# Up projections of a gated FFN as two-by-two blocks: seven products of half size in place of eight

## The chip, the cores and the metric

The kernel runs on one core of one Trainium2 chip, with its engines TensorE (PE in the profile), VectorE (DVE), ScalarE (ACT), GpSimd (POOL) and SyncE (SP, which issues most DMAs). The metric is device microseconds of one execution; runs are summed up by their median.

## The reference, cut to what matters

The program is a decoder trunk of two layers over 528 tokens (16 meta tokens and 512 real ones) of width 1024. Each layer is a token mixer (differential attention, then sparse attention with an indexer) followed by a gated FFN with a causal convolution of three taps. The FFN is the part that is changed:

```python
D_MODEL, FFN_HIDDEN, CONV_WIDTH = 1024, 2816, 3

def conv_ffn(h, w_up, conv_w, conv_b, w_down):      # h = rms_norm(stream, gain)
    u = h @ w_up                                    # 1024 x 5632
    T = u.shape[1]
    up = jnp.pad(u, ((0, 0), (CONV_WIDTH - 1, 0), (0, 0)))
    c = conv_b + sum(conv_w[j] * up[:, j:j + T] for j in range(CONV_WIDTH))
    g, val = jnp.split(c, 2, axis=-1)
    return (jax.nn.silu(g) * val) @ w_down          # 2816 x 1024
```

[...]

## The kernel before

Activations stand turned: 128 features on the partitions, 528 tokens along the free axis, so the stream h is eight tiles of 128 x 528. Every operand of a product is split into a rounded part and a rest (`two`, L392: ACT casts the high part, DVE or POOL subtracts it to get the low part), and a product is three matmuls: high by high, high by low, low by high. In the program's names the split weights are pairs wh and wl, or a lent pair of K tiles; the split activations are R tiles.

An up column is 128 columns of the weight: eight blocks of 128 x 128, each multiplied in three passes over two spans of tokens, 48 matmuls in all (`project`, L463). Column j of the gate half and column j of the value half make a pair; there are 22 pairs. `conv` (L924) takes a finished column out of PSUM: one DVE product with the row of inverse norms (tt<-ps,rbc), one ACT instruction for the last tap, two DVE instructions for the other taps (tt<-tt,cw,tt), then SiLU of the gate, the product of gate and value, and the split of the result into R tiles.

The columns come in three groups of 7, 7 and 8 pairs, and each is followed by its part of the down projection, eight products (`residual`, L699), whose PSUM result DVE adds to the stream (h<-ps,h). One pair of the next group is put ahead of each of the first two blocks of downs:

```python
order = ups[0] + ups[1][:2] + downs[0] + ups[1][2:] + ups[2][:2] + downs[1] + ups[2][2:] + downs[2]
```

What the text calls an up-block is the run of pairs between two blocks of downs: A (8 pairs), B (7) and C (7) in each layer.

A weight passes through two buffers. `loader` (L440) takes one of three raw tiles of 128 x 1024 and issues one DMA on the SP queue; `splitter` (L448) takes a wh/wl pair, casts and subtracts, and gives the raw tile back; `project` gives the pair back after its last matmul. There are two such pairs, and two more made of the attention's K tiles are lent while the FFN runs (`lend_keys`, L725). PSUM has four tiles of two banks, and columns take at most three of them (`PP`, L364).

The order on each engine is not written by hand. Tasks are generators with a priority; `Plan` (L192) emits the instruction that can start first by its own table of costs (`_cost`, L69) and keeps that order in the program. An instruction in an `Alt` may go to several engines, and the planner takes the one that ends first; `plan.bias` is added to DVE's end, and in the FFN it is `SPARE_FFN` (L52), 0 before the change, so that nearly all such instructions stand on DVE there.

## Time and profile before

| | |
|---|---|
| median of three runs | 1419.01 us (1418.5 to 1422.07) |
| the profiled execution | 1417.88 us, of which 1416.1 us lie between its first and last instruction |
| PE busy | 1372.6 us, 97% of the span, 10703 matmuls |
| DVE busy | 960.7 us, 68% |
| ACT busy | 679.9 us, 48% |
| POOL busy | 347.5 us, 25% |
| DMA | 124.33 MB, mean 88 GB/s |

The profile is of one execution. Busy time counts an instruction from its start to its end on its engine, waiting for a shared resource included; matmuls overlap, so their records are longer than their pace. A tile's name stands without its buffer number: tt is a work tile, ps a PSUM tile, raw and ns are tiles into which weights are loaded. In the trace every instruction has the line of the planner's emit (L270), so groups are told apart by tiles and shapes.

The two FFNs take the stretches from about 310 to 690 us and from about 1035 us to the end.

### The profile page before, as it was taken

The numbers are of one execution on the slowest core, as the hardware profiler recorded it, in microseconds if no ns is written. First come the engines' busy times: TensorE is split into PE (matmuls) and PEld (weight loads), VectorE is DVE, ScalarE is ACT, GpSimd is POOL, SyncE is SP. The second block draws the span as 40 slices with busy tenths as digits, with TensorE's granted clock in tenths as the row PEclk, the third lists the DMA queues.
The fourth block names the chain that finished last, engine by engine and source line by source line (L and its number), as shares of the span: only waits on it lengthen the run. The fifth ranks groups of instructions, "written<-read, shape, count | busy, mean of one in ns | idle before, by whom it ended". The sixth has DMA issues, their size and how long they took to land. (4 is left out here: it accounts for less than half of the span.)

```text
span 1416.1 us, 26368 instructions
## 1 busy us (share of the span) xinstructions
PE 1372.6 (97%) x10703; PEld 1331.9 (94%) x10703; DVE 960.7 (68%) x1659; ACT 679.9 (48%) x1260; POOL 347.5 (25%) x441
## 2 busy tenths in 40 slices
PE   8989999999999999999989989999999999999997
PEld 7888999999999999999989989898999989989997
DVE  6878767457645763775599988887666637646764
ACT  4566676434423432443356477777444324423454
POOL 1654654420000000000247764442310000000012
PEclk8999999999999999999999999999999999999999
DMA  6422233233233323332312331222333233333333
GB/s 178 103 61 61 76 91 103 57 96 90 81 95 94 87 82 102 90 90 70 90 45 75 83 96 49 69 68 76 94 90 97 80 104 92 91 101 90 90 113 111
DMA packets 223084, 124.33 MB, mean 88 GB/s; under 512 B 7001, under 2 KB 218338, under 8 KB 222962
## 3 DMA queue, kind: packets, MB, share of 16 engines
q1 hardware_dynamic: 219234, 111.89, 27.5%
q0 software_dynamic: 2560, 8.65, 2.9%
q10 hardware_dynamic: 1168, 2.10, 0.4%
q8 instruction: 84, 1.38, 0.4%
q14 instruction: 38, 0.31, 0.1%
HBM read 111.87 MB, written 2.10 MB: 80 GB/s over the span
## 5 line engine op out<-in xcount | busy, mean ns | idle before, releaser
L270 PE MATMUL ps<-R,wh 128*128 128x256 f32 (+4 forms) x4016 | 680.8, 289 | 1.6 <-POOL R L270 0.9
L270 PEld LDWEIGHTS ps<-R,wh 128*128 128x128 f32 (+1 forms) x4016 | 562.5, 189 | 9.4 <-POOL R L270 1.1
L270 PE MATMUL ps<-R,wl 128*128 128x272 f32 (+3 forms) x2008 | 424.4, 288 | 0.0
L270 PE MATMUL ps<-R,K 128*128 128x256 f32 (+3 forms) x3240 | 418.4, 289 | 0.0
L270 PEld LDWEIGHTS ps<-R,K 128*128 128x128 f32 x3240 | 405.6, 189 | 7.6
L270 PEld LDWEIGHTS ps<-R,wl 128*128 128x128 f32 x2008 | 312.2, 188 | 3.2
L270 ACT CAST wh<-raw 128x1024 fp32r<-128x1024 f32 (+3 forms) x173 | 145.6, 847 | 202.7 <-PE ps L270 147.6
L270 DVE TENSOR_TENSOR wl<-raw,wh 128x1024 fp32r<-128x1024 f32 (+3 forms) x128 | 139.9, 1096 | 23.6 <-ACT wh L270 21.8
L270 DVE TENSOR_TENSOR h<-ps,h 128x528 f32<-128x528 f32 (+3 forms) x70 | 45.7, 653 | 143.0 <-PE ps L270 143.0
L270 DVE TENSOR_TENSOR tt<-ps,rbc 128x528 f32<-128x528 f32 (+2 forms) x89 | 62.4, 701 | 114.9 <-PE ps L270 109.6
L270 DVE SCALAR_TENSOR_TENSOR tt<-tt,cw,tt 128x528 f32<-128x528 f32 (+1 forms) x176 | 133.4, 758 | 8.2 <-ACT tt L270 4.9
L270 ACT CAST K<-raw 128x1024 fp32r<-128x1024 f32 (+1 forms) x76 | 77.9, 1027 | 119.9 <-PE ps L270 105.5
L270 POOL TENSOR_TENSOR acc<-acc,tt 128x528 f32<-128x528 f32 (+1 forms) x22 | 36.2, 1645 | 400.6 <-ACT tt L270 400.6
L270 ACT CAST R<-tt 128x512 fp32r<-128x512 f32 (+2 forms) x84 | 48.5, 585 | 139.7 <-DVE tt L270 139.6
L270 DVE TENSOR_TENSOR K<-raw,K 128x1024 fp32r<-128x1024 f32 (+1 forms) x75 | 89.6, 1195 | 10.8 <-ACT K L270 9.3
L270 PE MATMUL ps<-K,X 128*128 128x272 f32 (+2 forms) x464 | 79.7, 308 | 11.0 <-DVE tt L270 5.6
L270 ACT ACTIVATE ns<-ns,st 128x528 f32<-128x528 f32 (+4 forms) x160 | 82.1, 514 | 13.6 <-DVE st L270 11.8
L270 POOL TENSOR_TENSOR wl<-raw,wh 128x512 fp32r<-128x512 f32 (+1 forms) x45 | 70.4, 1566 | 47.6 <-ACT wh L270 47.0
L270 PEld LDWEIGHTS ps<-K,X 128*128 128x128 f32 x464 | 65.6, 182 | 15.9 <-DVE st L270 3.9
L270 ACT ACTIVATE tt<-tt,cw 128x528 f32<-128x528 f32 (+1 forms) x88 | 72.3, 821 | 14.8 <-DVE tt L270 14.6
L270 POOL MEMSET tt<- 128x2 f32 x44 | 4.2, 99 | 302.2 <-DVE tt L270 302.2
L270 ACT ACTIVATE tt<-tt 128x528 f32<-128x528 f32 (+1 forms) x44 | 28.1, 639 | 81.8 <-DVE tt L270 81.7
(120 smaller groups left out, 1359.0 us busy)
## 6 DMA issues: line engine op xcount, KB each, us to landing
raw<-in_ffn_w_up_dram SPq DMA_DIRECT2D x88, 512.0 KB
raw<-in_ffn_w_down_dram SPq DMA_DIRECT2D x32, 448.0 KB
raw<-in_dsa_w_in_dram SPq DMA_DIRECT2D x28, 512.0 KB
raw<-in_da_w_qkv_dram SPq DMA_DIRECT2D x24, 512.0 KB
raw<-in_ffn_w_down_dram SPq DMA_DIRECT2D x22, 512.0 KB
K<-K POOLq DMA_DIRECT2D x32, 264.0 KB, 3.0
raw<-in_da_w_o_dram SPq DMA_DIRECT2D x8, 512.0 KB
raw<-in_dsa_w_o_dram SPq DMA_DIRECT2D x8, 512.0 KB
```

What stands on the lines that cost most here:

```text
L270: self.tc.keep_in_program_order(op.call(*op.a, **op.k))
```

## The change

Pairs 3 to 21 of each layer (`FIRST7 = 3`, so 19 of 22) are no longer two columns of 48 matmuls. The two inner halves of the weight's rows, by gate and value, are a two-by-two block matrix; the two inner halves of the features, by two halves of the tokens, are another. Their product is made of seven half-size products instead of eight (the variant with 4 sums of weight blocks, 4 of token blocks and 7 of the results). One half-size product is 12 matmuls over 264 tokens (260 in layer 1).

- Weights: `seven_slabs` loads the two columns as before, but keeps both raw tiles; POOL makes four sums of 128 x 512 (`sums`), two of them into Cr and Sr, which the FFN does not otherwise use. Seven blocks of 128 x 512 are then split in four steps (`two7`): ACT casts and DVE subtracts, as a scalar_tensor_tensor, which has no choice of engine.
- Tokens: `t_tiles` makes the four sums of token blocks once per layer, and splits them, in tiles that the attention no longer needs (pl, X, zt, K).
- Results: `sums7` adds up the seven PSUM results, one ACT copy and seven DVE additions of 128 x 264; the norm's factor is then applied from SBUF in `post7`, on POOL or DVE. The taps and what follows are as before (`taps`).
- Buffers: one lent wh/wl pair instead of two (a K tile and zv), so three pairs in all; three ns tiles are lent as raw tiles, so six. zv and zt are cleared or handed back for the next layer.
- `SPARE_FFN` goes from 0 to 600, which moves `Alt` instructions in the FFN from DVE to POOL.

```diff
-SPARE, SPARE_TAKEN, SPARE_FFN = 800.0, 600.0, 0.0
+SPARE, SPARE_TAKEN, SPARE_FFN = 800.0, 600.0, 600.0
+FIRST7 = 3
...
+    def seven_slabs(src_g, src_v):
...
+        def part_g(raw, wh, wl):
+            yield from two7(wh, wl, raw)
+
+        def part_s(raw, wh, wl):
+            yield summed[0]
+            for i, x in enumerate(mine["s"]):
+                yield from two7(wh[:, 512 * i:512 * i + 512], wl[:, 512 * i:512 * i + 512], x)
+            split_s.set()
+
+        def part_v(raw, wh, wl):
+            yield summed[1]
+            yield from two7(wh, wl, mine["v"])
+            RAW.put(mine["v"])
+
+        def part_4(raw, wh, wl):
+            yield summed[2]
+            yield from two7(wh[:, :512], wl[:, :512], mine["g"][:, 512:])
+            RAW.put(mine["g"])
...
+        def sums():
+            yield ld[ids[0]]
+            yield ld[ids[1]]
+            s12 = yield S12
+            mine["s"] = s1, s2 = s12
+            gr, vr = mine["g"], mine["v"]
+            yield g.tensor_tensor(out=s1, in0=vr[:, :512], in1=vr[:, 512:], op=ALU.add)
+            yield g.tensor_tensor(out=s2, in0=s1, in1=gr[:, :512], op=ALU.subtract)
+            summed[0].set()
+            yield g.tensor_tensor(out=vr[:, :512], in0=gr[:, :512], in1=vr[:, :512], op=ALU.subtract)
+            summed[1].set()
+            yield sp_[ids[0]]
+            yield g.tensor_tensor(out=gr[:, 512:], in0=gr[:, 512:], in1=s2, op=ALU.subtract)
+            summed[2].set()
+            yield split_s
+            S12.put(s12)
...
+    def two7(hi, lo, src):
+        yield s.copy(hi, src)
+        yield v.scalar_tensor_tensor(out=lo, in0=src, scalar=1.0, in1=hi.bitcast(F32), op0=ALU.mult, op1=ALU.subtract)
...
+    def product(o, w, c0, x, cut):
+
+        (wh, wl), (xh, xl) = w, x
+        n = cut[1] - cut[0]
+        yield [mm(o[:, :n], ww[:, c0 + k * P:c0 + k * P + P], y[k][:, cut[0]:cut[1]], k == 0 and j == 0, k == 3 and j == 2)
+               for k in range(4) for j, (ww, y) in enumerate(((wh, xh), (wh, xl), (wl, xh)))]
...
+        s0 = 0 if l == 0 else 8
+        half = (T - s0) // 2
+        n1, n2 = (s0, s0 + half), (s0 + half, T)
...
+        def t_tiles():
+            yield heads_done[l]
...
+            for k in range(4):
+                yield norm.ev[k]
+                yield norm.ev[k + 4]
+                ya, yb = yield TT, 2
+                for y, kk in ((ya, k), (yb, k + 4)):
+                    yield s.mul(y[:, s0:T], h[kk][:, s0:T], gcol[:, norm.g0 + kk:norm.g0 + kk + 1])
+                a, b = ([y[:, c[0]:c[1]] for c in (n1, n2)] for y in (ya, yb))
+                e = (g, v)
+                sub = lambda o, i0, i1: Alt([x.tensor_tensor(out=o, in0=i0, in1=i1, op=ALU.subtract) for x in e])
+                yield sub(a[0], a[1], a[0])
+                yield sub(a[1], b[1], a[1])
+                yield sub(b[1], b[1], a[0])
+                yield sub(b[0], b[1], b[0])
+                q = got[4 * k:4 * k + 4]
+                for i, y in enumerate((ya, yb)):
+                    yield from two7(q[2 * i][:, s0:T], q[2 * i + 1][:, s0:T], y[:, s0:T])
...
+        def sums7(gi, j, ps, ev):
...
+            add = lambda o, a, b, op=ALU.add: v.tensor_tensor(out=o, in0=a, in1=b, op=op)
+            yield ev[0]
+            yield s.copy(t, A(0))
+            yield add(c[0][0], B(0), t)
+            PP.put(ps[0])
+            yield ev[1]
+            yield add(t, A(1), t)
+            yield add(u4, B(1), t)
+            PP.put(ps[1])
+            yield ev[2]
+            yield add(c[1][1], A(2), u4)
+            yield add(t, A(2), t)
+            yield add(c[1][0], t, B(2), ALU.subtract)
+            PP.put(ps[2])
+            yield ev[3]
+            yield add(c[0][1], A(3), u4)
+            PP.put(ps[3])
...
+        def post7(gi, j, kind, U):
...
+            yield Alt([e.tensor_tensor(out=o, in0=o, in1=rbc[:, s0:], op=ALU.mult) for e in (g, v)])
+            c = yield TT
+            yield from taps(gi, j, kind, U, c, 0 if t0 == 0 else c0 - s0 - 2)
...
+        def up7(gi, j, wx):
...
+            for i, two_ in enumerate((((0, xs(0), n1), (512, xs(4), n1)),
+                                      ((512, ts(1), n2), (0, ts(0), n1)),
+                                      ((0, ts(0), n2), (512, ts(1), n1)),
+                                      ((0, xs(4), n2),))):
+                w = yield from weights(wx[i])
+                p = ps[i] = yield PP
+                for b, (cc, x, cut) in enumerate(two_):
+                    yield from product(p[:, 512 * b:], w, cc, x, cut)
+                WH.put(w)
+                ev[i].set()
...
+    def lend_tiles(l):
+        yield heads_done[l]
+        k = yield KS[0]
+        WH.lend(Guest(k))
+        for _ in range(3):
+            t = yield NS
+            raw = t[:, :1024]
+            ns_of[id(raw)] = t
+            RAW.lend(raw)
```

The order of the instructions shows what this does to DVE and POOL. The first place is DVE in up-block B of layer 0. Before, one pair reads so (wl and K are low parts of weights, rbc the row of inverse norms, cw_175 the taps of layer 0):

```order
L270 TENSOR_TENSOR tt_102<-ps_152,rbc 128x528
L270 TENSOR_TENSOR wl_115<-raw_113,wh_114 128x1024
L270 SCALAR_TENSOR_TENSOR tt_108<-tt_102,cw_175,tt_108 128x528 x2
L270 TENSOR_TENSOR tt_104<-ps_153,rbc 128x528
L270 TENSOR_TENSOR K_124<-raw_111,K_122 128x1024
L270 SCALAR_TENSOR_TENSOR tt_101<-tt_104,cw_175,tt_101 128x528 x2
L270 TENSOR_TENSOR tt_108<-tt_108,tt_101 128x528
L270 TENSOR_TENSOR R_92<-tt_108,R_90 128x528
```

Now the same stretch of DVE's queue holds, for about one pair:

```order
L271 SCALAR_TENSOR_TENSOR zv<-ns_126,K_122 128x1024
L271 SCALAR_TENSOR_TENSOR wl_115<-Cr,wh_114 128x512
L271 TENSOR_TENSOR tt_108<-ps_152,tt_103 128x264
L271 SCALAR_TENSOR_TENSOR wl_115<-Sr,wh_114 128x512
L271 TENSOR_TENSOR tt_103<-ps_152,tt_103 128x264
L271 SCALAR_TENSOR_TENSOR tt_109<-tt_110,cw_175,tt_109 128x528
L271 TENSOR_TENSOR tt_108<-tt_103,ps_152 128x264
L271 SCALAR_TENSOR_TENSOR wl_117<-ns_127,wh_116 128x1024
L271 SCALAR_TENSOR_TENSOR zv<-ns_126,K_122 128x512
L271 TENSOR_TENSOR tt_107<-ps_151,tt_103 128x264
L271 SCALAR_TENSOR_TENSOR tt_109<-tt_110,cw_175,tt_109 128x528
L271 SCALAR_TENSOR_TENSOR tt_105<-tt_102,cw_175,tt_105 128x528
```

The splits of the weights have grown from two of 1024 columns to five instructions (two of 1024 and three of 512 columns), the product with rbc is mostly gone, and additions of 264 columns out of PSUM stand between the splits and the taps.

The second place is POOL in the same up-block. Before, all that it holds there are these clearings of two columns:

```order
L270 MEMSET tt_106 128x2
L270 MEMSET tt_102 128x2
L270 MEMSET tt_101 128x2
L270 MEMSET tt_107 128x2
L270 MEMSET tt_105 128x2
```

Now it holds, for the same block, rows of this kind (Cr and Sr are the two sums of weight blocks, raw and ns the raw weights):

```order
L271 TENSOR_TENSOR Cr<-ns_126 128x512
L271 TENSOR_TENSOR tt_108<-tt_108,rbc 128x528
L271 TENSOR_TENSOR Sr<-Cr,ns_127 128x512
L271 TENSOR_TENSOR ns_126<-ns_127,ns_126 128x512
L271 TENSOR_TENSOR tt_102<-tt_102,tt_110 128x528
L271 TENSOR_TENSOR ns_127<-ns_127,Sr 128x512
L271 TENSOR_TENSOR Cr<-raw_113 128x512
L271 MEMSET tt_109 128x2
L271 MEMSET tt_105 128x2
L271 TENSOR_TENSOR Sr<-Cr,raw_111 128x512
L271 TENSOR_TENSOR raw_113<-raw_111,raw_113 128x512
```

Per pair there are four sums of 512 columns, about one and a half products with rbc, and part of the gate's product and of the split of the result.

The third place is DVE where up-block B ends and the downs begin:

```order
L271 TENSOR_TENSOR tt_109<-ps_152,tt_109 128x264
L271 SCALAR_TENSOR_TENSOR tt_104<-tt_106,cw_175,tt_104 128x528
L271 TENSOR_TENSOR tt_105<-tt_109,ps_152 128x264
L271 TENSOR_TENSOR tt_102<-ps_151,tt_109 128x264
L271 SCALAR_TENSOR_TENSOR tt_107<-tt_101,cw_175,tt_107 128x528
L271 TENSOR_TENSOR tt_102<-tt_102,rbc 128x528
L271 SCALAR_TENSOR_TENSOR tt_108<-tt_105,cw_175,tt_108 128x528
L271 SCALAR_TENSOR_TENSOR tt_110<-tt_102,cw_175,tt_110 128x528
L271 SCALAR_TENSOR_TENSOR tt_108<-tt_105,cw_175,tt_108 128x528
L271 SCALAR_TENSOR_TENSOR tt_110<-tt_102,cw_175,tt_110 128x528
L271 TENSOR_TENSOR h_61<-ps_153,h_61 128x528
L271 TENSOR_TENSOR wl_117<-ns_126,wh_116 128x896
```

The last additions of the pair that was put ahead of the downs, its product with rbc and its taps stand before the first addition to the stream (h_61<-ps_153,h_61). Two splits of down weights (896 columns) stand further up, and the third right behind that addition.

## Rows read from the trace of the kernel before

**Rows 1.** The page of the kernel before, busy time of each engine.

```profile
PE 1372.6 (97%) x10703; PEld 1331.9 (94%) x10703; DVE 960.7 (68%) x1659; ACT 679.9 (48%) x1260; POOL 347.5 (25%) x441
```

**Rows 2.** Stretches by engine: two in the first FFN, two in the second.

```profile
core 0: us, PE busy (x) PEld busy (x) DVE busy (x) ACT busy (x) POOL busy (x), PEclk, DMA share, GB/s
310.00:670.00 360.00, 360.00 (x2958) 360.00 (x2957) 217.33 (x265) 131.85 (x159) 4.86 (x42) 1.00 0.31 89
340.00:400.00 60.00, 60.00 (x495) 60.00 (x494) 41.37 (x53) 25.50 (x32) 1.09 (x11) 1.00 0.30 87
1040.00:1070.00 30.00, 30.00 (x255) 30.00 (x254) 22.34 (x29) 14.62 (x18) 0.00 (x0) 1.00 0.31 90
1360.00:1416.10 56.10, 48.44 (x369) 45.81 (x367) 28.91 (x40) 27.89 (x48) 14.66 (x13) 0.96 0.37 113
```

**Rows 3.** Timeline of PE: start, length; downs of the second FFN.

```profile
1130.59 9.88 PE L270 MATMUL ps<-R,K 128*128 128x512 f32 x42
```

**Rows 4.** DVE groups by form, 340 to 400 us: count, busy us, mean ns.

```profile
L270 DVE SCALAR_TENSOR_TENSOR tt<-tt,cw,tt 128x528 f32<-128x528 f32 x20 | 15.3, 767 | 0.5
...
L270 DVE TENSOR_TENSOR R<-tt,R 128x528 fp32r<-128x528 f32 x6 | 4.2, 708 | 4.2 <-ACT R L270 4.2
...
L270 DVE TENSOR_TENSOR wl<-raw,wh 128x1024 fp32r<-128x1024 f32 x3 | 3.7, 1225 | 0.5 <-ACT wh L270 0.5
L270 DVE TENSOR_TENSOR wl<-raw,wh 128x896 fp32r<-128x896 f32 x2 | 2.2, 1082 | 0.0
```

**Rows 5.** Groups by form, whole run.

```profile
L270 ACT CAST wh<-raw 128x1024 fp32r<-128x1024 f32 x82 | 86.1, 1050 | 135.0 <-PE ps L270 101.0 <-issue 33.8
...
L270 DVE SCALAR_TENSOR_TENSOR tt<-tt,cw,tt 128x512 f32<-128x512 f32 x88 | 66.0, 750 | 3.9 <-ACT tt L270 2.4
...
L270 POOL TENSOR_TENSOR wl<-raw,wh 128x512 fp32r<-128x512 f32 x37 | 50.9, 1378 | 42.6 <-ACT wh L270 42.1
...
L270 ACT CAST wh<-raw 128x512 fp32r<-128x512 f32 x72 | 43.6, 615 | 37.3 <-PE ps L270 17.7 <-issue 12.8 <-POOL R L270 3.6
...
L270 DVE CUSTOM_DVE_ANT_0 ns<-ps,mask 128x272 f32<-128x272 f32 x16 | 7.0, 436 | 0.0
```

**Rows 6.** Timeline of DVE around 44 us.

```profile
43.72 0.71 DVE L270 TENSOR_TENSOR tt<-tt,Sr 128x528 f32<-128x528 f32 x1
44.46 1.72 DVE L270 TENSOR_TENSOR X<-tt,X 64x528 fp32r<-64x528 f32 x1
46.21 1.72 DVE L270 TENSOR_TENSOR K<-tt,K 64x528 fp32r<-64x528 f32 x1
47.85 0.69 DVE L270 TENSOR_TENSOR tt<-ps,Cr 128x528 f32<-128x528 f32 x1
48.47 0.67 DVE L270 TENSOR_TENSOR wl<-raw,wh 128x512 fp32r<-128x512 f32 x1
49.17 1.78 DVE L270 TENSOR_TENSOR K<-tt,K 64x528 fp32r<-64x528 f32 x1
```

**Rows 7.** Timeline of POOL around 44 us.

```profile
43.81 1.80 POOL L270 TENSOR_TENSOR X<-tt,X 64x528 fp32r<-64x528 f32 x1 [1.38 <-DVE tt L270]
45.69 1.68 POOL L270 TENSOR_TENSOR tt<-tt,tt 128x528 f32<-128x528 f32 x1
...
49.07 1.32 POOL L270 TENSOR_TENSOR X<-tt,X 64x528 fp32r<-64x528 f32 x1
```

**Rows 8.** Timeline of DVE around 55 us, inputs from PSUM.

```profile
54.48 0.57 DVE L270 CUSTOM_DVE_ANT_0 ns<-ps,mask 128x400 f32<-128x400 f32 x1
...
54.97 0.44 DVE L270 CUSTOM_DVE_ANT_0 ns<-ps,mask 128x272 f32<-128x272 f32 x1
```

**Rows 9.** Timeline of POOL around 55 us.

```profile
54.08 1.31 POOL L270 TENSOR_TENSOR tt<-tt,tt 128x528 f32<-128x528 f32 x1 [2.13 <-issue]
55.36 1.28 POOL L270 TENSOR_TENSOR wl<-raw,wh 128x512 fp32r<-128x512 f32 x1
```

More of the change, by code (lines that the diff above doesn't have):

```diff
@@ L440, in loader @@
     def loader():
-        for load, _ in slabs:
+        for load, _, _ in slabs:
             yield loaded and x_in or x_half
-            raw = yield RAW
-            yield from load(raw)
+            raw = None
+            if load:
+                raw = yield RAW
+                yield from load(raw)
             loaded.append(raw)
@@ L461, in hybrid_trunk, with load, go @@
     SPANS = [(0, CUT), (CUT, T)]
+    S12 = Buf([(Cr[:, :512], Sr[:, :512])])
+    seven = []
+    def seven_slabs(src_g, src_v):
+        mine = {}
+        first = len(slabs)
+        def load(name, src):
+            def go(raw):
+                mine[name] = raw
+                yield sy.dma_start(out=raw.rearrange("p (k c) -> p k c", c=P), in_=src)
+            return go
+        def part_g(raw, wh, wl):
[13 more added lines that the diff above has]
+            RAW.put(mine["g"])
+        summed, split_s = [Event() for _ in range(3)], Event()
+        ids = [slab(load("g", src_g), part_g, True), slab(load("v", src_v), part_s, True),
+               slab(None, part_v, True), slab(None, part_4, True)]
+        def sums():
[14 more added lines that the diff above has]
+            S12.put(s12)
+        seven.append(sums)
+        return ids
@@ new lines, in two7, with all_sums @@
+    def two7(hi, lo, src):
+        yield s.copy(hi, src)
+        yield v.scalar_tensor_tensor(out=lo, in0=src, scalar=1.0, in1=hi.bitcast(F32), op0=ALU.mult, op1=ALU.subtract)
+    def all_sums():
+        for x in seven:
+            yield from x()
+    def product(o, w, c0, x, cut):
[3 more added lines that the diff above has]
+               for k in range(4) for j, (ww, y) in enumerate(((wh, xh), (wh, xl), (wl, xh)))]
@@ L903, in ffn @@
             downs[2][2:] = [(2, m, 0, hf) for hf in range(2) for m in range(2, KD)]
-        order = ups[0] + ups[1][:2] + downs[0] + ups[1][2:] + ups[2][:2] + downs[1] + ups[2][2:] + downs[2]
+        a1 = 1 if groups[1][0] >= FIRST7 else 2
+        order = ups[0] + ups[1][:a1] + downs[0] + ups[1][a1:] + ups[2][:1] + downs[1] + ups[2][1:] + downs[2]
         ws = []
         for x in order:
-            if len(x) == 3:
+            if len(x) == 3 and x[2] < 0:
+                ws.append(seven_slabs(*[wsrc(Wu, 0, KD, (x[1] + NF * kind) * P) for kind in range(2)]))
+            elif len(x) == 3:
                 ws.append(plain(wsrc(Wu, 0, KD, (x[1] + NF * x[2]) * P), KD))
@@ L934, in conv, with taps @@
             PP.put(ps)
+            yield from taps(gi, j, kind, U, c, f0)
+        def taps(gi, j, kind, U, c, f0):
+            m = j + NF * kind
             cv = c[:, :no]
@@ new lines, in t_back @@
+        def t_back():
+            for buf, ts in guests:
+                buf.put(*ts)
+            RAW.give_back(lambda t: NS.put(ns_of[id(t)]))
+        def sums7(gi, j, ps, ev):
+            U, W_, tmp = yield TT, 3
+            t, u4 = tmp[:, :half], tmp[:, half:2 * half]
+            u0 = 2 if t0 == 0 else 0
+            c = [[x[:, u0 + i * half:u0 + i * half + half] for i in range(2)] for x in (U, W_)]
+            if t0 == 0:
+                for x in (U, W_):
+                    yield g.memset(x[:, 0:2], 0.0)
+            A = lambda i: ps[i][:, :half]
+            B = lambda i: ps[i][:, 512:512 + half]
+            add = lambda o, a, b, op=ALU.add: v.tensor_tensor(out=o, in0=a, in1=b, op=op)
[15 more added lines that the diff above has]
+            PP.put(ps[3])
+            TT.put(tmp)
+            spawn(post7(gi, j, 0, U), 5)
+            spawn(post7(gi, j, 1, W_), 5)
@@ L969, in filler @@
             for x, wx in zip(order, ws):
-                if len(x) == 3:
+                if len(x) == 3 and x[2] < 0:
+                    yield from up7(x[0], x[1], wx)
+                elif len(x) == 3:
                     w = yield from weights(wx)
@@ L1450, in put @@
             NS.put(y)
+    for l in range(2):
+        spawn(lend_tiles(l), 0)
     n0, n1, n2, n3 = Norm(0), Norm(16), Norm(8), Norm(24)
```

73 lines of the change are left out of this document (53 added, 20 removed).

## The prediction, made before the changed kernel was run

> **What bounds the kernel now.** The first look is at the busy line of the page [rows 1]: PE is busy for 97% of the span, so work taken off PE shortens the run as long as nothing else becomes late. Next come the stretches by engine [rows 2]: inside the first FFN PE is busy for 360 of 360 us, DVE for 217, ACT for 132 and POOL for 4.86. The reader is to see three things there: PE has no gap to fill, DVE has 40% to spare, and POOL does nothing at all. The pace of PE follows from the same rows: 495 matmuls of 272 and 256 tokens in 60 us are 121 ns each, and 2958 in 360 us are 121.7; in the second FFN 255 of 260 and 256 in 30 us are 117.6. Downs there are matmuls of 512, 42 in 9.88 us [rows 3], 232 ns each with a small overlap at the end.
>
> Then the prices on the other engines. In the quiet stretch of the first FFN, with POOL idle, a DVE instruction with two inputs from SBUF costs 0.767 us (tap, 528 columns), 0.708 (split of 528), 1.225 (split of 1024) and 1.08 (896) [rows 4]. Last, and deciding, is how DVE and POOL share SBUF. Around 44 us both have such work [rows 6, 7]: POOL starts 0.09 us behind a DVE product of 0.71 us, and ends after 1.80 us where it takes 1.32 when it goes first; the DVE instructions that start behind POOL take 1.72, 1.72 and 1.78 us for work of 0.70, and each ends about 0.56 us after POOL's instruction has ended. So they take turns: one waits until the other has finished. A DVE instruction that reads PSUM doesn't take part: two of them take 0.57 us (400 columns) and 0.44 (272, the mean in rows 5) across a POOL instruction of 1.31 us that isn't lengthened either [rows 8, 9].
>
> **What PE loses.** A pair goes from 96 matmuls to 84. Layer 0: 12 x 121.7 ns x 19 pairs = 27.7 us (264 tokens are the mean of 272 and 256). Layer 1: 12 x 117.6 x 19 = 26.8, less 1.3 because 260 tokens stand where the mean was 258: 25.5. Together 53 us. That the twelve matmuls of a product go to one PSUM area one after the other costs nothing: the 512-token downs do the same and keep their pace [rows 3].
>
> **What DVE and POOL get, in up-block B of layer 0.** The order shows what stands on DVE between the last addition of the downs before and the first of the downs behind: 13 splits of 1024 columns, 19 of 512, 2 of 896, 28 taps, 9 other instructions of 528 with two SBUF inputs, and 49 additions of 264 columns out of PSUM. A split is now a scalar_tensor_tensor, which at 528 columns is 0.06 us dearer than the plain subtraction (0.767 against 0.708), so 1.285 us for 1024; for 512 there is a row of that form, 0.750 [rows 5]. An addition of 264 is nearest to the PSUM reduction of 272 columns, 0.436 [rows 5]; I take 0.43. Sum: 13 x 1.285 + 19 x 0.750 + 2 x 1.08 + 28 x 0.767 + 9 x 0.708 + 49 x 0.43 = 82 us. Neighbouring records overlap by 0.07 us (47.85 + 0.69 against 48.47) or leave 0.03 between them (43.72 + 0.71 against 44.46) [rows 6]; I take an overlap of 0.04, so 120 of them take 77 us.
>
> PE needs in the same stretch 7 x 84 x 0.1217 + 42 x 0.1217 = 76.7 us, the seven pairs and the first down. DVE alone would just keep up.
>
> POOL has 43 instructions there, 24 sums of 512, 18 of 528 and one of 896. The mean row for 512 is 1.378 us, with waits in it [rows 5]; undisturbed they are 1.28 and 1.31 [rows 9], so 57 us: POOL alone would keep up as well. But all 43 read two SBUF tiles, and so do 71 of DVE's 120. Each POOL instruction that isn't hidden beside an addition out of PSUM puts 1.02 us on DVE (1.72 less 0.70). The 49 additions are 21 us long and hide 16 POOL instructions at best; the other 27 cost 27.5 us. DVE then needs 105 us where PE needs 77.
>
> Some of this is absorbed: two splits of down weights stand in DVE's queue ahead of the first addition to the stream, so PE can do a second down while DVE finishes, 5.1 us. In the downs DVE needs 1.8 us per down (1.08 + 0.71) against PE's 5.1, and has caught up by their end, but can't run far ahead: a changed pair fills a wh/wl pair four times, and there are three. A split that waits for POOL's sum holds up what is queued behind it on DVE, the taps and the additions, and for these PE waits, since columns have three PSUM tiles. Block B thus costs 105 - 76.7 - 5.1 = 23 us.
>
> **The other blocks, by the same steps.** Block A of layer 0 (three plain pairs and five changed, token sums among them): DVE 84, PE 91, POOL 45 instructions of full length, 30 of them not hidden: 84 + 30.5 - 91 - 5 = 18. Block C: DVE 80, PE 77, 25 not hidden: 80 + 25.5 - 77 - 6 = 22. Layer 1, with 512 and 520 columns and PE's quicker pace: 19, 26 and 25. All six: 133 us. A bound from below is no collision at all, and then the blocks cost nothing; from above all POOL instructions collide, 16 x 1.02 more per block, 98 us in all.
>
> **What costs nothing.** ACT gets five casts per pair where it had two (2 x 1.05 + 3 x 0.615 us in place of 2.1, rows 5) and one PSUM copy: 19 x 2.3 = 44 us on top of 132 of 360. If ACT were late, the splits behind it would be. The DMAs are the same in number and size. The token sums lie beside the first three pairs, 35 us of PE work. The clearing of zv is one POOL instruction per layer, ahead of a stage that PE fills. The lent ns tiles only bring loads forward. PE's clock: where PE was idle for 14% of a stretch, at the end of the run, the granted clock was 0.96 [rows 2], so nearly always at the 2.4 GHz level; at worst the same 4% of 490 us in the up-blocks, 20 us, is lost, which goes to the upper end of the range.
>
> **The sum.** 1417.9 us (the profiled execution) - 53 + 133 = 1498. That execution is 1.1 us below the median of the runs, so I predict 1499.
>
> **A rule that prices it higher.** The rows show that a held DVE instruction ends 0.56 us after POOL's, less than its own 0.70 us, so its fixed part isn't repeated. The Trainium skill (SBUF — State Buffer, section "SBUF: two separate sides") says that the shared ports are an exclusive lock, which whoever starts first keeps for the whole instruction. That both wait fully agrees with the rows; that the whole length counts doesn't. What it would make of the time is the second rival.
>
> **Rivals.** *PE stays the bound.* POOL's work falls into stretches in which DVE adds out of PSUM or waits, and the blocks take PE's time: 1419 - 53 = 1366 us. For it: both engines, each by itself, fit into every block, and over a whole layer there is room. Against it: the two add up to 61 + 57 = 118 us of turns in block B, where PE offers 77. The place is the wait of a DVE split or tap behind a POOL sum; it decides the sign at 13 collisions of 43 per block, where (13 x 1.02 - 5 + 0.6) x 6 = 53. Its range is 1360 to 1400, its chance 0.21.
>
> *Every instruction waits for the other's whole length.* Then a block takes the sum of both, in B 61 + 57 = 118 us with the additions hidden, and 118 - 77 - 5 = 36 us are lost, 13 more than forecast: 1499 + 6 x 13 = 1577. It also stands for chains in which POOL, ACT and DVE wait for each other in turn. Chance 0.09.
>
> *Half of it is absorbed.* PE runs three downs ahead of DVE instead of one, 10 us less per block: 1439, and with a few more hidden POOL instructions 1400 to 1430. Against it: the third split stands behind the first addition. Chance 0.10, of which 0.04 fall on either side of no change by less than 0.3% (about what a measurement of this kernel can tell from none).
>
> **How the numbers follow.** The forecast, turns taken in the up-blocks, has a chance of 0.60; its own range is 1440 to 1570, from 10 us less per block to most POOL instructions colliding. The range of 1375 to 1575 takes in the absorbed case and the upper part of the first rival, and leaves out some 0.2, the rest of that rival and what lies above. Faster: 0.21 and 0.03 of the absorbed case, 0.24. Same: 0.04. Slower: 0.72.
>
> **What would show it.** Right: in the up-blocks PE is busy for 70 to 80% of the time, its idle time ended by DVE (PSUM not freed, weights not split); the 512-column splits on DVE have a mean near 1.1 us instead of 0.75, while additions out of PSUM stay at 0.43; POOL's 512 sums are above 1.4 us; DVE is busy for over 90% there; the downs run at PE's pace. Wrong: PE without gaps in blocks B and C, or DVE splits at 0.75 us with POOL at work; or gaps that ACT or a DMA ends.

## The result, and the profile after

The changed kernel takes **1562.93 us** (median of 4 runs, 1560.76 to 1565.07) against 1418.91 for the kernel before on the same chip: a ratio of 1.101, 95% interval 1.0987 to 1.1033. The forecast was 1499 us with a range of 1375 to 1575. The profiled execution took 1561.97 us, with a span of 1560.1, against 1417.88 and 1416.1: 144.1 us more.

The page's busy line after, which answers to [rows 1]:

```profile
PE 1378.2 (88%) x10247; PEld 1317.1 (84%) x10247; DVE 1223.8 (78%) x1936; ACT 770.2 (49%) x1443; POOL 820.8 (53%) x746
```

PE has 456 matmuls fewer, just 12 x 19 x 2, but is busy for longer than before, in a span that has grown by 144 us. So something stretches the matmuls, and something leaves gaps.

The stretches by engine after, answering to [rows 2]: the six up-blocks (A, B, C of the first FFN, then of the second), each from the last addition to the stream before it to the first one behind it. The columns are the stretch, its length, the busy time of PE, its weight loads, DVE, ACT and POOL, PE's granted clock, the DMAs' share and GB/s:

```profile
300.90:420.60 119.70, 98.68 (x762) 96.88 (x761) 107.60 (x127) 55.40 (x79) 66.38 (x60) 0.95 0.25 71
458.00:563.90 105.90, 84.47 (x631) 81.93 (x630) 100.26 (x121) 47.01 (x69) 68.79 (x51) 0.92 0.28 80
601.60:711.90 110.30, 92.30 (x680) 89.48 (x679) 101.74 (x125) 48.74 (x71) 66.95 (x53) 0.92 0.30 85
1102.40:1219.80 117.40, 97.35 (x738) 93.61 (x737) 105.69 (x125) 54.79 (x79) 72.38 (x46) 0.94 0.25 73
1255.10:1362.40 107.30, 82.01 (x610) 78.35 (x610) 102.48 (x122) 46.58 (x69) 64.63 (x38) 0.94 0.28 79
1398.50:1511.20 112.70, 89.21 (x634) 83.45 (x634) 102.32 (x123) 48.25 (x71) 65.40 (x39) 0.93 0.29 80
```

Before, the same blocks took 100.0, 87.2, 88.5, 97.5, 85.0 and 87.0 us. Now DVE is busy for 90 to 96% of each of them and PE for 76 to 84%. Block B of the first FFN, which the prediction worked out at 105 us, takes 105.9.

What DVE's instructions cost in that block, by form (count, busy us, mean ns, then DVE's idle time ahead of them and what ended it; fp32r is the program's rounded float32 type):

```profile
L271 DVE SCALAR_TENSOR_TENSOR tt<-tt,cw,tt 128x528 f32<-128x528 f32 x28 | 32.8, 1188 | 0.1
L271 DVE TENSOR_TENSOR tt<-ps,tt 128x264 f32<-128x264 f32 x42 | 17.5, 423 | 3.3 <-PE ps L271 2.3 <-ACT tt L271 0.6
L271 DVE SCALAR_TENSOR_TENSOR wl<-ns,wh 128x1024 fp32r<-128x1024 f32 x4 | 7.3, 1826 | 0.0
L271 DVE SCALAR_TENSOR_TENSOR wl<-raw,wh 128x512 fp32r<-128x512 f32 x4 | 4.7, 1169 | 0.0
```

And POOL's in the same block and columns:

```profile
L271 POOL TENSOR_TENSOR tt<-tt,rbc 128x528 f32<-128x528 f32 x10 | 15.3, 1543 | 10.2 <-DVE tt L271 10.2
L271 POOL TENSOR_TENSOR ns<-ns,Sr 128x512 f32<-128x512 f32 x3 | 4.8, 1597 | 0.0
L271 POOL TENSOR_TENSOR raw<-raw,raw 128x512 f32<-128x512 f32 x2 | 4.0, 1998 | 0.0
```

The taps have gone from 767 ns [rows 4] to 1188, a split of 512 columns to 1169, where the prediction took the 750 of a tap of that size [rows 5], and a POOL instruction from the 1.28 and 1.31 us of [rows 9] to between 1.5 and 2.0. The additions out of PSUM, at 423 ns, have not moved. One such turn on DVE and on POOL (start, length, instruction, idle time before it):

```profile
549.28 1.49 DVE L271 SCALAR_TENSOR_TENSOR tt<-tt,cw,tt 128x528 f32<-128x528 f32 x1
550.70 0.42 DVE L271 TENSOR_TENSOR tt<-ps,tt 128x264 f32<-128x264 f32 x1
551.04 2.31 DVE L271 SCALAR_TENSOR_TENSOR tt<-tt,cw,tt 128x528 f32<-128x528 f32 x1
```

```profile
548.16 2.05 POOL L271 TENSOR_TENSOR tt<-tt,tt 128x528 f32<-128x528 f32 x1 [0.71 <-PE ps L271]
550.16 2.62 POOL L271 TENSOR_TENSOR zv<-ns,K 128x896 fp32r<-128x896 f32 x1
```

The tap that starts at 551.04 ends at 553.35, 0.57 us after POOL's instruction has ended (552.78): the pattern of [rows 6, 7], with the addition out of PSUM at 550.70 untouched in between.

What PE waits for in block B, the four largest (total us, number of waits, longest):

```profile
PE ps L271 <- DVE tt L271: 8.0, 3, 4.1
PE ps L271 <- ACT R L271: 6.2, 1, 6.2
PE ps L271 <- DVE wl L271: 2.9, 2, 1.9
PE ps L271 <- DVE zv L271: 1.8, 3, 0.9
```

DVE ends 13.4 of the 21.5 us, ACT 7.2 and POOL 0.9. The wait for R is a wait for the result of the group's last pair. It falls within the first down:

```profile
560.92 0.81 PE L271 MATMUL ps<-R,wh 128*128 128x272 f32 x2 [6.15 <-ACT R L271]
```

And what the clock does around this gap, and in the rest of that block of downs (columns as in the stretches above):

```profile
558.00:568.00 10.00, 6.15 (x26) 5.85 (x27) 8.66 (x9) 4.30 (x6) 4.59 (x3) 0.51 0.05 16
568.00:601.60 33.60, 33.60 (x278) 33.60 (x277) 11.80 (x14) 6.31 (x8) 9.74 (x9) 1.00 0.27 79
```

PE stands idle from 554.77 to 560.92 us. From 558 to 568 it is granted the 1.2 GHz level (0.51), then 2.4 GHz again. Before, PE had no gap there [rows 2].

**Where the 144 us are.** PE's matmul records give a balance. In quiet stretches their starts stand 118 ns apart behind one of 256 columns, 120 behind 260, 121.5 behind 264, 125 behind 272, 232 behind 512 (and 109 behind 128, taken as it is). Each matmul, counted at the quiet spacing of its width, is *work*. What the measured spacing exceeds that by is lost. Where the trace's record of the clock shows the 1.2 GHz level, the loss counts as *clock*, up to once the quiet spacing; all the rest counts as *stalls*. In us, before and after:

| | work | clock | stalls |
|---|---|---|---|
| first attention with its out-projection | 262.0, 262.3 | 6.4, 6.4 | 29.6, 30.5 |
| six up-blocks | 543.9, 497.9 | 0.0, 27.3 | 1.0, 148.8 |
| six blocks of downs | 219.4, 211.5 | 0.0, 8.9 | 0.4, 0.5 |
| second attention with its out-projection | 312.0, 312.4 | 4.2, 5.8 | 25.5, 35.4 |
| whole program | 1339.1, 1285.9 | 10.7, 48.3 | 57.5, 215.9 |

(The rows leave out the end of the program, which is the same.) So PE has 53.2 us less work, loses 37.6 more to its clock and 158.4 more to stalls, 142.8 in sum; 1.2 of the rest is time ahead of the first matmul and behind the last. Below, *clock* and *stalls* are these sums for a whole program.

### The profile page after: what moved, and what is told of

It reads as the page before. It is cut to its first block, busy times and chain, and to the rows that moved or that the text cites. A ratio compares the mean times of both kernels' runs of the same rounds, so it can differ in the third digit from the quotient of the medians.

```text
span 1560.1 us, 26538 instructions
## 1 busy us (share of the span) xinstructions
PE 1378.2 (88%) x10247; PEld 1317.1 (84%) x10247; DVE 1223.8 (78%) x1936; ACT 770.2 (49%) x1443; POOL 820.8 (53%) x746
## 4 chain that ended last, share of the span: by engine, by line
PE 41%; DVE 27%; POOL 6%; issue 5%; ACT 3%; DVEq 0%; POOLq 0%; ACTq 0%
PE ps L271 41%; DVE tt L271 12%; DVE wl L271 6%; POOL tt L271 4%; DVE zv L271 3%; DVE acc L271 3%; DVE st L271 2%; ACT tt L271 1%; ACT R L271 1%; ACT wh L271 1%; POOL R L271 1%; POOL acc L271 1%; DVE R L271 0%; DVE X L271 0%; DVE ns L271 0%
## 5 line engine op out<-in xcount | busy, mean ns | idle before, releaser
L271 PE MATMUL ps<-R,wh 128*128 128x256 f32 (+5 forms) x3716 | 660.9, 293 | 44.4 <-ACT R L271 34.7
L271 PEld LDWEIGHTS ps<-R,wh 128*128 128x128 f32 (+1 forms) x3716 | 538.7, 190 | 59.7 <-ACT R L271 37.6
L271 PE MATMUL ps<-R,wl 128*128 128x272 f32 (+4 forms) x1858 | 426.1, 291 | 11.6 <-DVE wl L271 9.7
L271 PE MATMUL ps<-R,K 128*128 128x256 f32 (+4 forms) x940 | 189.4, 312 | 2.1 <-ACT K L271 2.1
L271 ACT CAST wh<-raw 128x512 fp32r<-128x512 f32 (+3 forms) x164 | 130.7, 803 | 120.9 <-PE ps L271 82.6
L271 PEld LDWEIGHTS ps<-R,K 128*128 128x128 f32 x940 | 152.5, 204 | 7.9 <-ACT K L271 2.5
L271 DVE TENSOR_TENSOR tt<-ps,tt 128x264 f32<-128x264 f32 (+3 forms) x260 | 117.0, 456 | 35.1 <-PE ps L271 20.5
L271 PE MATMUL ps<-R,zv 128*128 128x272 f32 (+4 forms) x470 | 126.8, 313 | 13.5 <-DVE zv L271 13.3
L271 POOL TENSOR_TENSOR R<-tt,R 128x528 fp32r<-128x528 f32 (+2 forms) x60 | 86.1, 1437 | 85.8 <-ACT R L271 80.9
L271 POOL TENSOR_TENSOR tt<-tt,tt 128x528 f32<-128x528 f32 (+3 forms) x57 | 91.6, 1607 | 57.5 <-DVE tt L271 28.4
L271 PEld LDWEIGHTS ps<-R,zv 128*128 128x128 f32 x470 | 86.4, 203 | 18.3 <-DVE zv L271 15.1
```

The costliest lines, as they stand in the source:

```text
L271: self.tc.keep_in_program_order(op.call(*op.a, **op.k))
```

## The experiments

**Is it the turns, with nothing else changed?** Two edits of the kernel before that leave the queues of PE, DVE and ACT as they are. In `conv`, behind the product with rbc:

```diff
+            spawn(pool_work(U), 5)
...
+        def pool_work(U):
+            pace = g.tensor_tensor(out=acc[2][:, :2], in0=U[:, 4:6], in1=U[:, 4:6], op=ALU.add)
+            ops = [g.tensor_tensor(out=Cr[:, :512], in0=Cr[:, :512], in1=Sr[:, :512], op=ALU.subtract) for _ in range(4)]
...
+            yield [pace] + ops
```

> The kernel before, with five idle-running POOL instructions for each up column: one of 2 columns that waits for the column's U (the pace), then four subtractions Cr - Sr of 512 columns, 1.3 us each, whose result nothing reads. PE, DVE, ACT and the DMAs do what they did, in the same order. POOL gets 14 x (4 x 1.3 + 0.25) = 76 us in an up-block of 87, DVE has 58 us there, some 50 instructions with two SBUF inputs among them. Theory (turns): each of these can lose up to 1.02 us, 50 us at most, so DVE needs 80 to 105 us where PE needs 87: 5 to 15 us more per block, about 1419 + 6 x 10 = 1480 us (1440 to 1510), taps of 512 and 528 columns at 1.2 to 1.7 us instead of 0.76, and additions or products that read PSUM as before. Rival (POOL costs DVE nothing, the changed kernel is slow by its own chains): 1419, taps at 0.76.

and, as its control, with the list of operations replaced:

```diff
-            ops = [g.tensor_tensor(out=Cr[:, :512], in0=Cr[:, :512], in1=Sr[:, :512], op=ALU.subtract) for _ in range(4)]
+            ops = [g.memset(acc[3], 0.0) for _ in range(12)]
```

> The control for the run before it: the same pace instruction, and in place of the four subtractions twelve clearings of a 128x400 tile, 0.43 us each, so POOL is at work as long (76 us per up-block) but reads no SBUF tile. Theory (turns, only where POOL reads two tiles): 1419 us as before, within 4 us, taps at 0.76. Rival (any POOL work on SBUF holds DVE): as slow as the run with the subtractions, about 1480.

The first takes **1536.30 us** (ratio 1.0831, 1.0815 to 1.0847), 118 us more than before; the second **1419.62** (1.001, 1.0001 to 1.002). Block B of the second FFN in the first, a stretch by engine, then groups of DVE and POOL by form (columns as above):

```profile
1237.60:1346.70 109.10, 99.86 (x741) 94.61 (x740) 93.37 (x71) 32.52 (x42) 99.42 (x69) 0.95 0.24 70
```

```profile
L270 DVE SCALAR_TENSOR_TENSOR tt<-tt,cw,tt 128x512 f32<-128x512 f32 x28 | 41.7, 1489 | 0.5
...
L270 DVE TENSOR_TENSOR tt<-ps,rbc 128x516 f32<-128x516 f32 x14 | 9.6, 684 | 4.0 <-PE ps L270 4.0
```

```profile
L270 POOL TENSOR_TENSOR Cr<-Cr,Sr 128x512 f32<-128x512 f32 x55 | 89.8, 1633 | 3.2
```

The same block in the control:

```profile
1160.00:1245.00 85.00, 85.00 (x694) 84.04 (x694) 56.26 (x71) 34.27 (x42) 69.08 (x165) 1.00 0.31 90
```

```profile
L270 DVE SCALAR_TENSOR_TENSOR tt<-tt,cw,tt 128x512 f32<-128x512 f32 x28 | 21.0, 750 | 0.5
L270 DVE TENSOR_TENSOR tt<-ps,rbc 128x516 f32<-128x516 f32 x14 | 9.7, 695 | 20.5 <-PE ps L270 15.5 <-POOL acc L270 4.8
```

DVE does the same 71 instructions in both, in 93.4 us against 56.3. That is 37.1 us for the 55 sums that POOL does beside them, 0.67 each. The taps take 1489 ns against 750, and the products that read PSUM 684 against 695, no difference. POOL at work for 69 us with clearings costs nothing. So what holds DVE is POOL reading SBUF beside DVE instructions that read two SBUF tiles, and this alone, with none of the two-by-two products in the kernel, is worth 118 us here. By the balance above some 93 of them are stalls and some 25 PE's clock, with PE's queue as it was. The longest waits are for the R tiles of last pairs, as in the changed kernel, so the turns alone can make those late (all waits of this kind in the run, their number, the longest):

```profile
PE ps L270 <- ACT R L270: 62.1, 9, 11.6
```

The loss was over the range that I gave for it: the taps' 1.2 to 1.7 us were right, but 10 us more per block became some 20. The Trainium skill (SBUF — State Buffer, section "SBUF: two separate sides") names just this pair, a DVE operation with two SBUF inputs against a GpSimd operation that reads SBUF, and the two runs agree with it: 1489 ns against 750.

**How much of the changed kernel's loss is the weight sums' turns?** POOL stays as long at work but hardly reads, every other queue is the same:

```diff
+        def short(full, o, a, b, op):
+            small = g.tensor_tensor(out=o[:, :2], in0=a[:, :2], in1=b[:, :2], op=op)
+            clears = [g.memset(acc[3], 0.0) for _ in range(3)]
...
+            return clears + [small]
...
-            yield g.tensor_tensor(out=s1, in0=vr[:, :512], in1=vr[:, 512:], op=ALU.add)
+            yield pool_sum(out=s1, in0=vr[:, :512], in1=vr[:, 512:], op=ALU.add)
...
```

(`pool_sum` passes a sum through `short`; the other three sums likewise. What is left out are the sums beyond their first two columns.)

> The changed kernel, with each of POOL's 4 x 19 x 2 weight sums cut to 2 columns and three clearings of a free 128x400 tile put ahead of it (0.43 us each, 1.3 us together), so POOL is as long at work and every other engine's instructions and order stay the same, but POOL reads next to nothing. Left out: the weight sums beyond their first 2 columns. Theory (turns: DVE waits where both read two SBUF tiles): in block B of layer 0 only POOL's other 19 instructions can still collide, 16 of them beside additions out of PSUM, so the block falls from 106 us to 80 to 85, all six blocks lose some 25 each, and the whole comes to about 1562 - 6 x 25 = 1410 us (1395 to 1450). Rival 1 (DVE is overloaded by its own work): no change, 1562. Rival 2 (the chain weight sum, cast, split is late, and four weight sets are filled per pair): POOL is as long at work, so no change, 1562. Rival 3 (PE's clock alone): the clock stays at 0.92 to 0.95 in the blocks, no change.

**1486.67 us** (1.0476, 1.0462 to 1.049): 76 less than the changed kernel, where I expected 150 (1395 to 1450). Block B, by engine:

```profile
450.40:542.40 92.00, 80.45 (x633) 78.13 (x632) 84.80 (x122) 46.69 (x69) 63.23 (x111) 0.96 0.33 92
```

DVE's time falls from 100.3 to 84.8, 15.5 us for the 21 sums that POOL does in it, 0.74 each. In the same block POOL's clearings and short sums take 35.1 us, where the full sums took 36.3, so POOL is as long at work. All three rivals (a DVE overloaded by its own work, POOL's length in the chain, the clock alone) had no change; each falls as the only cause. But stalls remain (154.0, from 215.9; clock 35.1, from 48.3): block B should have come down to 80 to 85, and what PE waits for there shows one reason why it did not:

```profile
PE ps L271 <- ACT R L271: 6.1, 1, 6.1
PE ps L271 <- DVE tt L271: 1.6, 2, 1.3
PE ps L271 <- DVE wl L271: 1.3, 3, 0.7
```

The wait for the last pair's R is as long as in the changed kernel (6.2 there). The next two runs ask whether it is a cost of its own; the prediction had none for it.

**The late last pair.** One edit puts two changed pairs ahead of the downs:

```diff
-        order = ups[0] + ups[1][:a1] + downs[0] + ups[1][a1:] + ups[2][:1] + downs[1] + ups[2][1:] + downs[2]
+        order = ups[0] + ups[1][:2] + downs[0] + ups[1][2:] + ups[2][:2] + downs[1] + ups[2][2:] + downs[2]
```

> The changed kernel with two changed pairs in place of one put ahead of the downs of the first and second group, 10.2 us more of PE work between a group's last pair and its downs. Theory (turns, and the last pair's chain of sums, products with rbc, taps, gate and split on a loaded DVE is late for the downs): the wait of 6 us for R in the first down and the half clock behind it go at four of the six downs, 4 x (6 + 5), and DVE's arrears are made up beside the downs, so about 1562 - 40 = 1522 us (1510 to 1545). Rival (DVE's total work per block sets the time wherever PE stands): the wait only moves to the next up-block, 1555 to 1565.

**1526.53 us** (1.0765, 1.0749 to 1.0781), 36 less than the changed kernel, within the theory's range, and the rival's 1555 to 1565 is out. But the sum behind the 40 us is only half right. Stalls fall from 215.9 to 179.6, 36 us in place of the 24 in the sum, and the clock's loss, which was to give the other part, does not fall (49.7). PE's waits for R over the whole run, in the changed kernel and here:

```profile
PE ps L271 <- ACT R L271: 34.7, 8, 6.9
```

```profile
PE ps L271 <- ACT R L271: 7.9, 3, 2.9
```

At the first down behind block B there is no wait for R left; from 530 to 575 us PE waits only for this:

```profile
PE ps L271 <- DVE wl L271: 2.2, 1, 2.2
PE ps L271 <- DVE tt L271: 1.3, 1, 1.3
```

The two edits together:

> The two edits together: POOL's weight sums cut to 2 columns with clearings ahead of them, and two changed pairs ahead of the downs. Left out: the weight sums beyond their first 2 columns. Theory (turns at DVE and the late last pair are separate costs): the gains add, 76 + 36, about 1562 - 112 = 1450 us (1440 to 1462). Rival (one cost seen twice: the last pair is late only because of the turns, or a DVE that catches up beside the downs makes the turns harmless): the second edit brings little on top of the first, 1475 to 1487.

**1446.67 us** (1.02, 1.0186 to 1.0214). PE, DVE and ACT have the same instructions in the same order as with two pairs ahead alone. The gains add: 76.3 + 36.4 = 112.7 were to be expected, 116.3 are measured. So the sums' turns and the late last pair are two costs. Stalls are 119.0 now, the clock's loss 28.8. The largest wait that is left is for weights that DVE has not split yet:

```profile
PE ps L271 <- DVE wl L271: 16.2, 13, 3.1
```

**The clock.** Is what PE loses at 1.2 GHz a matter of the gap ahead of the downs?

```diff
+        def keep_busy():
+            ps = yield SC
+            x = norm.xh[0]
+            fill = [mm(ps[:, :264], x[:, 16:16 + P], x[:, 16:280], True, True) for _ in range(48)]
...
                 elif x[0] < 2:
+                    if x[1] == 0:
+                        yield from keep_busy()
                     yield from down(x, wx)
...
+            yield from keep_busy()
             norm.free()
```

> The changed kernel, with 48 matmuls of 264 columns, whose result nothing reads, between the last product of an up-block and the first down, 5.8 us on PE at full clock: the wait of 6 us for the group's last R tiles in the first down stays, but PE works through it. Theory (the gap there drops PE's clock to half for some 10 us at the start of the downs): the six half-clock stretches at the downs go, 25 to 30 us less, about 1535 us (1530 to 1548), mean granted clock 0.97 or more. Rival 1 (the clock falls because PE has gaps all through the up-blocks): the stretches stay, 1560 to 1570. Rival 2 (PE has no spare time there, the wait moves with it): 6 x 5.8 more, 1597.

**1556.98 us** (1.0978, 1.0962 to 1.0995): 6 less than the changed kernel instead of 25 to 30. The downs behind blocks A and B of the first FFN, then block A itself and block A of the second FFN, by engine:

```profile
427.50:462.30 34.80, 34.80 (x288) 34.80 (x287) 13.17 (x16) 7.04 (x10) 11.09 (x10) 1.00 0.27 77
568.10:603.60 35.50, 35.50 (x294) 35.50 (x293) 14.05 (x17) 8.37 (x11) 10.34 (x10) 1.00 0.25 75
```

```profile
306.30:427.50 121.20, 107.44 (x816) 106.01 (x815) 107.43 (x127) 55.72 (x79) 66.39 (x60) 0.93 0.25 70
...
1105.00:1222.00 117.00, 104.33 (x790) 101.68 (x789) 105.09 (x125) 54.87 (x79) 72.88 (x46) 0.94 0.26 73
```

In five of the six blocks of downs the granted clock is 1.00 again (0.96 in the sixth), and their loss falls from 8.9 us to 1.1. That the dummy work went into the gap is plain from the time, which did not grow by the 35 us that the dummy matmuls take. But the up-blocks lose as much as before the edit, 28.4 us against 27.3, though the gap at their end is filled: the low clock there does not hang on that gap, and comes with the stalls all through the blocks, as the first rival has it, though the time lies 3 us under its range. The attentions, whose queues the edit leaves alone, lost 7 us more in this execution (19.4 against 12.2), so that the program's sum is the same, 48.7. One execution can't tell why, but that sum moves by itself: with the clearings above, in attentions that the edit doesn't touch, it is some 4 us, against 10.6 before. What the gap ahead of the downs costs by the clock is thus some 8 us and not the 25 to 30 of the theory; which of the stalls inside a block bring the clock down is not settled.

**Moving the work off POOL.** The weight sums on DVE:

```diff
-            yield g.tensor_tensor(out=s1, in0=vr[:, :512], in1=vr[:, 512:], op=ALU.add)
+            yield v.tensor_tensor(out=s1, in0=vr[:, :512], in1=vr[:, 512:], op=ALU.add)
...
```

> The changed kernel, with the four weight sums of a pair on DVE instead of POOL. Theory (turns): block B of layer 0 has 24 POOL instructions less; DVE gets 24 x 0.69 = 16.6 us of its own on top of 77 and keeps at most 3 collisions, 97 us in place of 106: some 8 us less per block, about 1562 - 50 = 1512 us (1490 to 1535), with DVE above 95% busy and its 512 splits near 0.75 us. Rival 1 (DVE overloaded by its own work): 16.6 us more per block, about 1660. Rival 2 (POOL's sums come late in the chain): the sums get shorter (0.69 in place of 1.3 to 2.3 us), so faster too, but DVE would show idle time ended by ACT or a DMA.

**1574.61 us** (1.1101, 1.1085 to 1.1117), a miss for the theory and both rivals: 12 more than the changed kernel. And the products with rbc and the like back on DVE where the planner sees room:

```diff
-SPARE, SPARE_TAKEN, SPARE_FFN = 800.0, 600.0, 600.0
+SPARE, SPARE_TAKEN, SPARE_FFN = 800.0, 600.0, 0.0
```

> The changed kernel with the planner's allowance for POOL in the FFNs back at 0: the instructions of 528 columns that may go to either engine (the products with rbc and the like) go to DVE where the planner thinks DVE is as early, the weight sums stay on POOL. Theory (turns): each instruction of 1.4 us moved off POOL takes 0.71 us of DVE and saves 1.02 where it collided: 10 to 18 per block, so 3 to 5 us less per block, 1530 to 1545 us. Rival 1 (DVE overloaded): 0.7 x 15 = 10 us more per block, 1620. Rival 2 (chain): no clear change, within 10 us of 1562.

**1558.86 us** (1.0983, 1.0968 to 1.0998), 4 less than the changed kernel, where the theory had 1530 to 1545.

With the sums on DVE, DVE is busy in block B for 100.2 us, as long as with the sums on POOL (100.3). The stretch by engine and two of DVE's groups (columns as above):

```profile
462.60:571.40 108.80, 86.74 (x634) 85.31 (x633) 100.16 (x139) 48.71 (x70) 35.55 (x33) 0.90 0.27 78
```

```profile
L271 DVE TENSOR_TENSOR ns<-ns,Sr 128x512 f32<-128x512 f32 x3 | 3.2, 1059 | 0.0
L271 DVE TENSOR_TENSOR Cr<-raw 128x512 f32<-128x512 f32 x3 | 2.0, 678 | 0.0
```

Undisturbed a sum takes DVE 0.68 us, and some groups have a mean of 1.06 beside what POOL still does; on POOL it costs DVE 0.74. Wherever the sums stand, DVE pays about as much. I had put 1.02 us against 0.69, the price of a collision that nothing hides, and so saw a gain that isn't there. That explains why nothing was gained, but not the 12 us more. By the balance those are PE's clock: the stalls are some 6 us less than in the changed kernel, and the clock's loss is some 20 us more (0.90 in block B, from 0.92).

The other run says little about a price, because its edit moved little. Of the 17 instructions of 528 columns that POOL does in block B of the changed kernel, 12 are still there, and 9 of the 10 products with rbc:

```profile
L271 POOL TENSOR_TENSOR tt<-tt,rbc 128x528 f32<-128x528 f32 x9 | 10.9, 1225 | 20.8 <-DVE tt L271 20.8
```

I had reckoned with 10 to 18 that move. The time lies where the second rival (the chain) put it, but the run can't tell that rival from an edit that does next to nothing.

**Fewer pairs.** Every second pair from the fourth on, 10 in place of 19:

```diff
-SPARE, SPARE_TAKEN, SPARE_FFN = 800.0, 600.0, 600.0
-FIRST7 = 3
+SPARE, SPARE_TAKEN, SPARE_FFN = 800.0, 600.0, 0.0
+SEVEN = range(3, 22, 2)
...
-        ups = [[(gi, j, -1) if j >= FIRST7 else (gi, j, kind) for j in grp for kind in range(1 if j >= FIRST7 else 2)]
+        ups = [[(gi, j, -1) if j in SEVEN else (gi, j, kind) for j in grp for kind in range(1 if j in SEVEN else 2)]
...
```

> The changed kernel with only every second pair from the fourth on changed (10 of 22 in place of 19), and the planner's allowance for POOL in the FFNs back at 0. PE loses 10 x 12 x 2 matmuls, 27.5 us. Theory (turns): per block 3 to 4 changed pairs bring about 14 weight sums on POOL, and DVE has 58 of 87 us of its own work and the additional 9 us, so 67 + 14 x 1.02 = 82 at most, which is within PE's 80 to 83: PE stays the bound, 1391 to 1400 us, faster than both. Rival 1 (DVE overloaded by its own work, no turns): the same or better, 1391. Rival 2 (chain: a changed pair starves PE by itself, whatever the load on DVE is): half of the loss stays, 1419 + 72 = 1491. Rival 3 (clock): any gap ahead of a block of downs still costs its half clock, 1400 to 1430.

**1441.07 us** (1.0159, 1.0145 to 1.0173): in none of the ranges, 41 us over the theory's. Work is 1311.1 (28.0 less than before), the clock's loss 14.7, but stalls are 104.3. In the blocks B there is hardly one (1.8 and 2.7 us); blocks A have 8 us each and blocks C 7 and 9. Block A of the first FFN, what PE waits for:

```profile
PE ps L271 <- POOL acc L271: 2.8, 1, 2.8
PE ps L271 <- POOL tt L271: 1.9, 1, 1.9
```

The sums of squares for the norm (acc) and its factors come late from POOL: the token sums stand ahead of them there. And in the blocks C, whose last pair (21) is a changed one, PE waits for R again, 1.7 and 2.4 us. So the last edit takes eight pairs, the third group's last one plain, and starts the token sums only when the norm's factors are there:

```diff
...
+SEVEN = (5, 7, 9, 11, 13, 16, 18, 20)
...
         def t_tiles():
...
+            yield e_r
             for k in range(4):
```

> 8 of 22 pairs changed (5, 7, 9, 11, 13, 16, 18, 20, so the last pair of the third group is a plain one), the token sums made only once the norm's factor is there (they stood ahead of its sums of squares on POOL, 5 us of waits per layer where every second pair was changed), the planner's allowance for POOL kept in the first FFN alone. PE loses 8 x 12 x 2 matmuls, 23 us. Theory (with half of the load on DVE and POOL what is left are those two waits): against the run with every second pair, 1441, 10 us less for the token sums, 5 less for the last pair, 6 more for two pairs fewer: 1432 us (1420 to 1440), still not faster than before, since the attention stages keep some 10 us of new waits. Rival (the waits come from DVE's load in general): 1441 to 1450.

> The same with the planner's allowance for POOL at 0 in both FFNs, as in the run with every second pair. Theory: 1432 us (1420 to 1440). If the allowance moves waits in the attention stages (30 us of PE's stalls ahead of the first FFN with it, 35 to 37 without), 5 us more than the run before it.

**1432.75 us** with the allowance in the first FFN (1.0105, 1.0091 to 1.0119) and **1422.58** without it (1.003, 1.0018 to 1.0042). Both lie in the theory's range, but the second was put at 5 us more than the first and takes 10 less. The waits for acc are gone, blocks A stall for 3.1 and 3.5 us in the second, its clock loses 9.8 us in all (10.7 before). PE has 22.4 us less work, and the stalls take more than all of it: 85.0 against 57.5, with some 17 of the difference in the up-blocks and some 10 in the attentions. That is the best version found, and it is still about 4.6 us over the kernel before.

## Why the prediction was right, and where it was not

**PE's gain** was put at 53 us; 53.2 measured.

**The turns** were right as a mechanism: DVE becomes what bounds the up-blocks, its instructions with two SBUF tiles and POOL's wait for each other, and additions out of PSUM don't take part. Most of the signs that were named came true: splits of 512 at 1.0 to 1.2 us, additions at 0.42, POOL's sums above 1.4, DVE at 90% and more; PE is busy for 76 to 84% of the up-blocks, where 70 to 80 were named and three of the six lie above. Two did not. The downs don't run at PE's pace (granted clock 0.94 to 0.97), and ACT ends 7.2 of the 21.5 us of waits in block B, which was named as a sign of being wrong: it is the chain of the last pair. The price was about right: 27 of 43 instructions at 1.02 us are 0.64 per POOL instruction, and a weight sum costs 0.74. That block B, where DVE was put at 105 us, takes 105.9 is in part luck: DVE is busy for 100.3 of them and idle for the rest.

**What was absorbed** was not as put. The second down that PE was to do ahead doesn't come: PE waits in its first down for the last pair's R, 6.2 us. The six blocks were put at 133 us after some 5 us off each, so at about 163 without; the up-blocks' stalls are 148. The long chain of the last pair, ahead of which only one pair stands, had no term.

**The step that failed in the sum** is "what costs nothing: PE's clock, at worst 20 us". It costs 36.2 us in the FFNs (27.3 in the up-blocks, 8.9 in the downs, none before) and 37.6 in all. The row behind it, a clock of 0.96 in a stretch with 14% idle time [rows 2], was taken for the worst case, and put into the range alone. The up-blocks, with 16 to 24% idle time, were granted 0.92 to 0.95, and the low level reaches into the downs behind them, which the prediction had at full pace.

**The token sums** "beside the first three pairs" were not free: they hold up the norm's own sums on POOL, 4.7 us of waits in block A of the first FFN.

**The second attention** was given no term and stalls for 10 us more. With eight pairs it is 5 (30.4 against 25.5), and 2.5 are there in the control with the clearings (28.0), which changes nothing in that stage. Whether the rest is the tiles that are lent or the order that the planner makes of it was not tried.

Put together: 1417.9 - 53.2 + 147.9 of stalls in the FFNs + 36.2 of clock + 12.4 in the attentions = 1561.2, against 1562.0 measured. The miss of 64 us is 15 in the blocks, 36 in the clock and 12 in the attentions. All three lie on the same side. That 1563 us are within the range owes something to its width: it spans 200 us and holds faster and slower results alike, and 1563 is 12 below its upper end.

**The rivals.** That PE stays the bound is refuted by every block. That each instruction waits for the other's whole length is refuted too, though its 1577 us stood nearer: it had 36 us for block B, which stalls for 25, and a held tap of 0.77 us ends 0.57 us after POOL's instruction. That half is absorbed did not come true either: PE does not get one down ahead, much less three. The nearest run, with two pairs ahead, gave 36 us, not the 60 to 99 of this rival.

What is left open: the 119 us of stalls that remain with neither the sums' reads nor the late pair, 61 over before. Some 50 of them are in the up-blocks. POOL's products, gates and splits (17 instructions of 528 columns in block B) still take turns there, the waits for acc and in the second attention are in it, and the largest wait is for split weights (wl, 16.2 us). Whether those are late because of DVE, of the three wh/wl pairs that each changed pair fills four times, or of the order that the planner chose was not tried.

## What to carry to other kernels

Before work goes to an idle POOL, look at what DVE does beside it: with two SBUF inputs on both sides, and DVE nearly full, an instruction on POOL cost DVE here about what it would cost on DVE itself (0.74 us against 0.68), so POOL's idle time was no room. The gain on PE was lost where another engine's length in the same stretch came near PE's new one, so compare the two before you take work off PE. Once PE had gaps, its clock was a term of its own, here a quarter of the loss. And where a chain gets longer, look at the place where PE must have its end: here more work put ahead of that place gave back 36 us.

## What the runs showed of the hardware that was not expected

Clearings on POOL, which only write SBUF, did not hold DVE at all: 152 of 433 ns each in a block of 85 us left the taps at 750 ns. And keeping PE at work through its longest gaps brought the clock of the downs behind them back to 1.00 in five blocks of six, but the loss of the up-blocks stayed (28.4 us against 27.3): there it does not hang on the longest wait alone, and which of the others bring it is open.
